# First sweep of a PEER encoder kernel: one 512-column matmul in place of two of 256, the halves added afterwards

## The chip, the cores and the metric

The kernel runs on one core of one Trainium2 chip. The metric is device time in microseconds (us) of one execution. Three runs of the kernel before gave 1670.82, 1672.67 and 1672.75 us, a median of 1672.67 us. Engines are named as the profile names them: PE (TensorE matmul), PEld (its weight load), DVE (VectorE), ACT (ScalarE), POOL (GpSimd), SP (SyncE, which issues the plain loads).

## The reference

One encoder layer over 256 tokens of 2048 values, all in float32: a norm, an input projection, two kinds of attention, an output projection, and then a PEER layer, which is what this case is about. Each token picks 8 x 16 of 16384 experts by two short searches, takes the dot product of its normed row with each chosen expert's row of `peer_u`, puts it through gelu, weighs it, and sums rows of `peer_v`:

```python
q = (xt @ w_query).reshape(n_tok, PEER_HEADS, 2, PEER_QUERY_DIM // 2)
scores = jnp.einsum('thcd,hcnd->thcn', q, sub_keys)
s_top, i_top = lax.top_k(scores, PEER_TOPK)
cand = s_top[:, :, 0, :, None] + s_top[:, :, 1, None, :]
best, pos = lax.top_k(cand.reshape(...), PEER_TOPK)
u = jnp.take(expert_u, eb, axis=0)
act = jax.nn.gelu(jnp.einsum('td,thkd->thk', xb, u))
return jnp.einsum('thk,thkd->td', act * gb, vv)
```

## The kernel before

Float32 products are made of three matmuls on rounded parts. An operand `w` is split by ACT into `hi`, its rounded high part, and by DVE into `lo = w - hi`; a product is `hi*h_hi + hi*h_lo + lo*h_hi`. `load_split` (line 165) takes one unit of 128 x 1024 values: a load of 512 KB on SP's queue, the ACT copy (L169, `hi`) and the DVE subtraction (L170, `lo`). `hi` and `lo` have three buffers each, so the split of a unit waits until PE has finished the unit three before it. Loads go to five raw buffers, three of their own and two in a part of the large array `A` that isn't in use yet.

The kernel is a chain of stages: projections and attention, the query projection (four groups), the first sweep, an extraction stage, the second sweep, the end.

The first sweep (from line 777) multiplies the first 1536 of the 2048 dimensions of all 16384 rows of `peer_u` with all 256 tokens. It has 192 units of 8 blocks of 128 x 128. A group `e` of 128 experts has KA = 12 blocks, so it lasts one and a half units; there are 128 groups. For each block three matmuls of 256 columns run one after the other (L790, L791, L792). `h_hi` and `h_lo` lie side by side in the tile `hTa[:, k]`, 2 x 256 values. Two groups share one PSUM bank (`both`), and when the odd one of a pair is done ACT copies the 512 sums into `A[:, e // 2]` (L795), where the two groups of a pair alternate.

The other 512 dimensions are fetched, not swept: for each token and each chosen expert a "dot" gathers a 2 KB row per partition with an indirect DMA by POOL (L644) and multiplies and sums it on DVE (L650). There are 256 dots. They can start once a query group's search is done. The searches themselves (top 16 of 128, pairs, top 16 of the pairs, decoding) are DVE steps, put in between.

DVE's order is written out by hand in this stretch (`manual_schedule`): per unit first the `lo` subtraction, then whatever `advance()` hands out. `advance()` (called once a unit) gives the searches a share of each unit: the work left divided by the units left until unit SEARCHED, but at most `rate` and at least MIN_S = 1.0, in its own cost units; the dots get what is left of `rate`:

```python
rate = max(rate, RATE)
share = max(min(rate, todo / max(SEARCHED - st["unit"], 1)), MIN_S) if todo else 0
```

Unit 0 of the sweep is unit 33 in that count. Before the searches are done the dots have four row buffers (`wm`). When they are done (`selected`), eight more are opened at once in pairs 52 to 59 of `A`, whose space the searches have used until then. Each buffer in `A` is closed four units before the sweep writes its pair. The row buffers are taken in turn from a queue; a newly opened one is put at its front.

After the sweep, the extraction stage reads all of `A` from its first matmul on (L838).

Of the kernel before, what the change touches and what calls it, by code (L numbers as in the profile page):

```python
# [13 lines left out]
AF = mybir.ActivationFunctionType  # L14
OP = mybir.AluOpType
# [3 lines left out]
P = 128  # L19
D = 2048  # L20
S = 256
# [14 lines left out]
KA = D1 // P  # L36
# [7 lines left out]
WORK = 14016  # L44
SEARCH = 22.0
DOT = 0.67
SEARCHED = 95
MIN_S = 1.0
RATE = 1.42
TAIL = 5  # L50
# [4 lines left out]
PAIRS = (52, 60)  # L55
# [47 lines left out]
def encoder_layer_kernel(ctx: ExitStack, tc: tile.TileContext, x, gT, w_in, gq, gk, w_out, g2,  # L103
                         w_query, sub_keys, u_head, u_tail, v_head, v_tail, gf, cst, rope, bias_a, out):
    nc = tc.nc
# [8 lines left out]
    A = consts.tile([P, NK // 2, S, 2], F32, name="A")  # L114
    arena = A.rearrange("p a b c -> p (a b c)")
    ha_pool = ctx.enter_context(ExitStack())
    hb_pool = ctx.enter_context(ExitStack())
    hTa = ha_pool.enter_context(tc.tile_pool(name="ha", bufs=1)).tile([P, KA, 2, S], F32R, name="hTa")
    hTb = hb_pool.enter_context(tc.tile_pool(name="hb", bufs=1)).tile([P, KD - KA, 2, S], F32R, name="hTb")

    def hTs(k, part, r):
        return hTa[:, k, part, r] if k < KA else hTb[:, k - KA, part, r]
# [15 lines left out]
    def mm_bank(name="mm"):  # L138
        return psm.tile([P, 512], F32, name=name, tag="mm")

    def at_bank(name="at"):
        return psa.tile([P, 512], F32, name=name, tag="at")
# [15 lines left out]
    def load_raw(src):  # L158
        raw = raw_tile("raw")[:, :src.shape[-1]]
        nc.sync.dma_start(raw, src)  # L160
        return raw
# [3 lines left out]
    def load_split(src):  # L165
        raw = loaded.popleft() if loaded else load_raw(src)
        hi, lo = (wp.tile([P, 1024], F32R, name=s, tag=s, bufs=3)[:, :raw.shape[-1]] for s in ("hi", "lo"))
        with tc.high_priority(AHEAD):
            nc.scalar.activation(hi, raw, AF.Copy)  # L169
            nc.vector.tensor_tensor(lo, raw, hi.bitcast(F32), op=OP.subtract)  # L170
        return hi, lo
# [91 lines left out]
    def project(xT, unit, order, background=None):  # L263

        ps = [mm_bank(f"pr{t}") for t in range(NT)]
        for n, i in enumerate(order):
            hi, lo = load_split(unit(i))
            for kk in range(2):
                k = 2 * i + kk
                c = slice(kk * 512, (kk + 1) * 512)  # L270
                first, last = n == 0 and kk == 0, n == len(order) - 1 and kk == 1
                for t in range(NT):
                    r = slice(t * P, (t + 1) * P)
                    nc.tensor.matmul(ps[t], xT(k, 0, r), hi[:, c], start=first, stop=False)  # L274
                    nc.tensor.matmul(ps[t], xT(k, 0, r), lo[:, c], start=False, stop=False)  # L275
                    nc.tensor.matmul(ps[t], xT(k, 1, r), hi[:, c], start=False, stop=last)  # L276
            if background:
                background()
        return ps
# [110 lines left out]
    def w_in_group(g, background=tick):  # L390
        return project(hTs, lambda i: w_in[g, i], W_OUT_ORDER if g == 5 else range(KD // 2), background)
# [3 lines left out]
    def enter():  # L395
        if entries:
            gained_.append(entries.popleft())
            transpose_gain(0, *gained_[-1])

    def split_entered():  # L400
        if gained_:
            t, c = gained_.popleft()
            split_rows(4 * c, 4, slice(t * P, (t + 1) * P))

    with tc.manual_schedule(engines={DVE}):
        for step in (enter, enter, split_entered, split_entered, enter):
            step()
        ps = w_in_group(8, lambda: (split_entered(), enter()))
# [11 lines left out]
    with tc.manual_schedule(engines={PE}):  # L420
# [58 lines left out]
        for g in range(4):  # L479
            ps = project(hTs, lambda i: w_out[g, i], W_OUT_ORDER, tick)  # L480
# [160 lines left out]
    spares = Ring([arena[:, i:i + DT] for i in range(SPARE * S, NK * S, DT)])  # L641
# [45 lines left out]
    def advance():  # L687
        st = state
        st["unit"] += 1
        while known and known[0][0] <= st["unit"]:  # L690
            g = known.popleft()[1]
            dotq.extend((t, 32 * g + j) for t in range(NT) for j in range(32))
        todo = sum(c for c, *_ in searches) + (4 - st["groups"]) * SEARCH
        rate = (todo + DOT * (NT * P - st["dots"])) / max(last_unit - st["unit"], 1)
        if todo:
            rate = max(rate, RATE)
        share = max(min(rate, todo / max(SEARCHED - st["unit"], 1)), MIN_S) if todo else 0
        st["s"] += share
        st["d"] += max(rate - share, 0)
        if not dotq:  # L700
            st["s"] += st["d"]
            st["d"] = 0.0
        while searches and st["s"] >= searches[0][0]:
            cost, fn, *args = searches.popleft()
            fn(*args)
            st["s"] -= cost
        if not searches:
            st["d"] += max(st["s"], 0) if dotq else 0
            st["s"] = 0.0
        while dotq and (st["d"] >= DOT or st["unit"] >= last_unit):  # L710
            dot(*dotq.popleft())
            st["dots"] += 1
            st["d"] -= DOT

    query = ctx.enter_context(ExitStack())
    for g in range(4):
        if g == 1:
            query.enter_context(tc.manual_schedule(engines={DVE}))
        ps = project(hTs, lambda i: w_query[g, i], QUERY_ORDER, advance if g else None)
# [10 lines left out]
    spares = Slots()  # L730
# [8 lines left out]
    def select_transposed(t):  # L739
        rows_ = sel.rearrange("p c g (t h) k -> p c t g (h k)", t=NT)[:, :, t]  # L740
        flat = seln[:, t]
        for c in range(3):
            nc.scalar.activation(flat[:, c].rearrange("p (g j) -> p g j", g=4), rows_[:, c], AF.Copy)
        nc.sync.dma_start(i1d[t * P:(t + 1) * P], flat[:, 0])
        tp = at_bank("seltp")
        for c in range(3):
            nc.tensor.transpose(tp[:, c * P:(c + 1) * P], flat[:, c], ident)
        for c, dst in enumerate((I1T, I2T, GT)):
            nc.scalar.activation(dst[:, t * P:(t + 1) * P], tp[:, c * P:(c + 1) * P], AF.Copy)

    units = NK * KA // 8
    both = None
    partT, actT, wT, wN = (h2t[:, i // 2, i % 2 * S:i % 2 * S + S] for i in range(4))
    wN = wN.rearrange("p (t j) -> p t j", t=NT)
    rootT = part.rearrange("p t j -> p (t j)")
# [3 lines left out]
    def rows_at(q):  # L759

        bc = wp.tile([P, 1024], F32, name="bc", tag="raw", bufs=RAW)
        nc.sync.dma_start(bc, bass.AP(tensor=i1d.tensor, offset=i1d.offset + 4 * q * P, ap=[[0, P], [1, 8 * P]]))
        rows[q // 2] = bc
# [12 lines left out]
    selected = False  # L776
    with query:
        for i in range(units):
            if i == SPARE * KA // 8 - 2:
                del raws[1]  # L780
            hi, lo = load_split(u_head[i])
            for b in range(8):
                e, k = divmod(8 * i + b, KA)
                c = slice(b * P, (b + 1) * P)
                if k == 0:
                    if e % 2 == 0:
                        both = mm_bank("act")
                    ps = both[:, e % 2 * S:e % 2 * S + S]
                h_hi, h_lo = hTs(k, 0, slice(0, S)), hTs(k, 1, slice(0, S))
                nc.tensor.matmul(ps, hi[:, c], h_hi, start=k == 0, stop=False)  # L790
                nc.tensor.matmul(ps, hi[:, c], h_lo, start=False, stop=False)  # L791
                nc.tensor.matmul(ps, lo[:, c], h_hi, start=False, stop=k == KA - 1)  # L792
                if k == KA - 1 and e % 2:
                    with tc.high_priority(FIRST):
                        nc.scalar.activation(A[:, e // 2], both.rearrange("p (c t) -> p t c", c=2), AF.Copy)  # L795
            advance()
            if not searches and not selected:
                selected = True
                for t in range(NT):
                    select_transposed(t)  # L800

                for p in range(PAIRS[1] - 1, PAIRS[0] - 1, -1):
                    spares.add(arena[:, p * 512:(p + 1) * 512], 2 * p * KA // 8 - 4)
            spares.now = i + 1
            if i == READY:
                tp = at_bank("parttp")
                for t in range(NT):
                    nc.tensor.transpose(tp[:, t * P:(t + 1) * P], part[:, t], ident)
                nc.scalar.activation(partT, tp[:, :S], AF.Copy)
                tp = at_bank("roottp")  # L810
                for t in range(NT):
                    nc.tensor.matmul(tp[:, t * P:(t + 1) * P], roots[:, NT + t:NT + t + 1].to_broadcast([P, P]), ident,
                                     start=True, stop=True)
                nc.scalar.activation(rootT, tp[:, :S], AF.Copy)
            if i == units - 1:
                for q in range(0, FULL, 2):
                    rows_at(q)
                for q in range(FULL):
                    hot_at(q)()
# [78 lines left out]
    units = NK * VC // 2  # L898
# [230 lines left out]
```

## Time and profile before

| | |
|---|---|
| median of three runs | 1672.67 us |
| profiled execution | 1670.96 us |
| its span, first to last instruction | 1669.1 us |
| granted TensorE clock, mean | 0.995 |
| PE busy | 1641.6 us (98%) |
| DVE busy | 1319.0 us (79%) |
| ACT busy | 852.9 us (51%) |
| POOL busy | 694.4 us (42%) |
| first sweep, first to last start of L790 | 441.8 to 1008.7 us |

The profiled execution takes 1.9 us more than its span. Busy time of matmuls is modelled at their ends, and matmuls overlap in it, so what a matmul costs in a stream is read from the distance between two starts and not from its duration. Shares of busy time are means over stages with different limits.

### The profile page before, as it was taken

The page shows a single profiled execution, that of the slowest core. Times are in us where ns is not written, and L with a number is a line of the kernel's source. Part 1 is how long each engine was busy: PE and PEld are TensorE (multiplying, and loading weights), DVE is VectorE, ACT ScalarE, POOL GpSimd, SP SyncE. Part 2 cuts the span into 40 slices and gives each one's busy share as a digit, 9 for nine tenths or more (in the row PEclk, how much of TensorE's full clock was granted, in tenths as well). Part 3 has the DMA queues.
Part 4 walks back from the last instruction along what each step waited for, and adds up shares of the span by engine and source line. Part 5 has one row for each costly group of instructions (what it writes and reads, how often), then busy time and mean ns, then how long its engine had stood idle before and what let it go on. Part 6 is the DMA issues. An engine that isn't in the chain of part 4 may idle for free.

```text
span 1669.1 us, 28381 instructions
## 1 busy us (share of the span) xinstructions
PE 1641.6 (98%) x10242; PEld 1489.6 (89%) x10242; DVE 1319.0 (79%) x2902; ACT 852.9 (51%) x1191; POOL 694.4 (42%) x582
## 2 busy tenths in 40 slices
PE   8999999999999999999999999999999999999997
PEld 6888888888899989999999999998888888888886
DVE  6665565569799967777777767997989999999996
ACT  6565564454444434444444448996444444444445
POOL 0000000001223366766765532334777666666661
PEclk9999999999999989999999999999999999999999
DMA  7644565666677789999999973335999999999994
GB/s 254 194 142 153 172 202 164 180 212 211 224 246 235 240 291 325 339 324 335 329 333 310 311 252 130 126 118 183 353 395 363 360 355 344 359 348 357 349 355 151
DMA packets 126173, 443.23 MB, mean 266 GB/s; under 512 B 17744, under 2 KB 18640, under 8 KB 125648
## 3 DMA queue, kind: packets, MB, share of 16 engines
q1 hardware_dynamic: 85072, 298.78, 52.6%
q0 software_dynamic: 40960, 142.64, 24.1%
q8 instruction: 80, 1.31, 0.3%
q14 instruction: 61, 0.50, 0.1%
HBM read 437.02 MB, written 4.33 MB: 264 GB/s over the span
## 4 chain that ended last, share of the span: by engine, by line
PE 92%; DVE 4%; ACT 2%; DMA 1%; issue 1%; SPq 0%; ACTq 0%; DVEq 0%
PE act L791 11%; PE act L790 11%; PE act L792 11%; PE o L924 10%; PE o L925 10%; PE o L923 10%; PE pr L276 6%; PE pr L275 6%; PE pr L274 6%; PE X L838 3%; PE W L888 3%; DVE lo L170 1%; PE o1p L844 1%; PE sc L356 1%; PE po L387 1%
## 5 line engine op out<-in xcount | busy, mean ns | idle before, releaser
L169 ACT ACTIVATE hi<-raw 128x1024 fp32r<-128x1024 f32 (+1 forms) x445 | 464.7, 1045 | 596.6 <-PE o L925 243.1
L170 DVE TENSOR_TENSOR lo<-raw,hi 128x1024 fp32r<-128x1024 f32 (+1 forms) x445 | 535.8, 1204 | 216.5 <-ACT hi L169 189.6
L790 PE MATMUL act<-hTa,hi 128*128 128x256 f32 x1536 | 436.7, 284 | 1.8 <-issue 1.8
L791 PE MATMUL act<-hTa,hi 128*128 128x256 f32 x1536 | 436.7, 284 | 1.8 <-issue 1.8
L792 PE MATMUL act<-hTa,lo 128*128 128x256 f32 x1536 | 436.6, 284 | 0.0
L644 POOL DMA_INDIRECT rows<-in_v_tail_dram,experts x256 | 325.5, 1272 | 152.4 <-DVE vsum L996 88.1
L644 POOL DMA_INDIRECT A<-in_u_tail_dram,experts x131 | 151.2, 1154 | 499.9 <-DVE den L636 408.4
L790 PEld LDWEIGHTS act<-hTa,hi 128*128 128x128 f32 x1536 | 296.6, 193 | 1.6 <-issue 1.5
L792 PEld LDWEIGHTS act<-hTa,lo 128*128 128x128 f32 x1536 | 296.6, 193 | 1.6 <-issue 1.6
L791 PEld LDWEIGHTS act<-hTa,hi 128*128 128x128 f32 x1536 | 296.6, 193 | 1.2 <-issue 1.2
L924 PE MATMUL o<-lo,wt 128*128 128x512 f32 (+1 forms) x768 | 293.5, 382 | 1.0 <-DVE lo L170 0.9
L923 PE MATMUL o<-hi,wt 128*128 128x512 f32 (+1 forms) x768 | 293.5, 382 | 0.9 <-ACT hi L169 0.9
L925 PE MATMUL o<-hi,wt 128*128 128x512 f32 (+1 forms) x768 | 293.2, 382 | 0.0
L644 POOL DMA_INDIRECT wm<-in_u_tail_dram,experts x125 | 160.6, 1285 | 169.1 <-DVE wm L650 120.8
L996 DVE SCALAR_TENSOR_TENSOR vsum<-rows,h2t,vsum 128x576 f32<-128x576 f32 x256 | 208.6, 815 | 11.3 <-DMA rows<-in_v_tail_dram,experts 8.5
L924 PEld LDWEIGHTS o<-lo,wt 128*128 128x128 f32 x768 | 144.3, 188 | 26.0 <-DVE lo L170 1.8
L923 PEld LDWEIGHTS o<-hi,wt 128*128 128x128 f32 x768 | 144.3, 188 | 25.3 <-ACT hi L169 1.4
L925 PEld LDWEIGHTS o<-hi,wt 128*128 128x128 f32 x768 | 144.2, 188 | 24.3 <-DVE wt L918 0.6
L274 PE MATMUL pr<-hi,hTa 128*128 128x512 f32 x408 | 164.3, 404 | 0.0
L275 PE MATMUL pr<-lo,hTa 128*128 128x512 f32 x408 | 160.0, 392 | 0.4 <-DVE lo L170 0.2
L276 PE MATMUL pr<-hi,hTa 128*128 128x512 f32 x408 | 159.6, 391 | 0.0
L169 ACT ACTIVATE hi<-A 128x1024 fp32r<-128x1024 f32 x72 | 76.4, 1062 | 127.5 <-PE act L791 71.1
(160 smaller groups left out, 2073.9 us busy)
## 6 DMA issues: line engine op xcount, KB each, us to landing
raw<-in_v_head_dram SPq DMA_DIRECT2D x128, 512.0 KB
raw<-in_u_head_dram SPq DMA_DIRECT2D x120, 512.0 KB
raw<-in_w_in_dram SPq DMA_DIRECT2D x72, 512.0 KB
A<-in_u_head_dram SPq DMA_DIRECT2D x72, 512.0 KB
raw<-in_v_head_dram SPq DMA_DIRECT2D x64, 448.0 KB
raw<-in_w_out_dram SPq DMA_DIRECT2D x32, 512.0 KB
raw<-in_w_query_dram SPq DMA_DIRECT2D x32, 512.0 KB
bc<-i1d SPq DMA_DIRECT2D x32, 512.0 KB
```

The source lines that it names most:

```text
L169: nc.scalar.activation(hi, raw, AF.Copy)
L170: nc.vector.tensor_tensor(lo, raw, hi.bitcast(F32), op=OP.subtract)
L274: nc.tensor.matmul(ps[t], xT(k, 0, r), hi[:, c], start=first, stop=False)
L275: nc.tensor.matmul(ps[t], xT(k, 0, r), lo[:, c], start=False, stop=False)
L276: nc.tensor.matmul(ps[t], xT(k, 1, r), hi[:, c], start=False, stop=last)
L644: nc.gpsimd.indirect_dma_start(out=rows_, out_offset=None, in_=table, in_offset=bass.IndirectOffsetOnAxis(ap=experts[:, j // 32, t * 32 + ...
L790: nc.tensor.matmul(ps, hi[:, c], h_hi, start=k == 0, stop=False)
L791: nc.tensor.matmul(ps, hi[:, c], h_lo, start=False, stop=False)
L792: nc.tensor.matmul(ps, lo[:, c], h_hi, start=False, stop=k == KA - 1)
L923: nc.tensor.matmul(ps, w[:, 0, r], hi[:, c], start=e == 0, stop=False)
L924: nc.tensor.matmul(ps, w[:, 0, r], lo[:, c], start=False, stop=False)
L925: nc.tensor.matmul(ps, w[:, 1, r], hi[:, c], start=False, stop=e == NK - 1)
```

## The change

- In the first sweep the two matmuls that use the same `hi` block become one of 512 columns over `h_hi` and `h_lo` side by side. The left half of the bank collects `hi*h_hi`, the right half `hi*h_lo`.
- Within a unit, for each group, all 512-column matmuls come first, then the `lo` matmuls of 256 columns, which add to the left half.
- A group has a bank of its own (128 in turn from four, in place of 64). ACT copies the left half (256 values, every second place of `A[:, e // 2]`).
- DVE adds the right half to it in place, three units after the unit in which the group ended, behind that unit's `lo` subtraction and ahead of `advance()`. In the last unit all that are left are added.
- The eight row buffers are opened one in every second unit, from the unit on in which the searches are done.
- SEARCHED goes from 95 to 101.

```diff
-SEARCHED = 95
+SEARCHED = 101
...
-                if k == 0:
-                    if e % 2 == 0:
-                        both = mm_bank("act")
-                    ps = both[:, e % 2 * S:e % 2 * S + S]
-                h_hi, h_lo = hTs(k, 0, slice(0, S)), hTs(k, 1, slice(0, S))
-                nc.tensor.matmul(ps, hi[:, c], h_hi, start=k == 0, stop=False)
-                nc.tensor.matmul(ps, hi[:, c], h_lo, start=False, stop=False)
-                nc.tensor.matmul(ps, lo[:, c], h_hi, start=False, stop=k == KA - 1)
-                if k == KA - 1 and e % 2:
+                blocks.setdefault(e, []).append((k, slice(b * P, (b + 1) * P)))
+            for e, ks in blocks.items():
+                if ks[0][0] == 0:
+                    ps = mm_bank("act")
+                for k, c in ks:
+                    h = (hTa[:, k] if k < KA else hTb[:, k - KA]).rearrange("p a t -> p (a t)")
+                    nc.tensor.matmul(ps, hi[:, c], h, start=k == 0, stop=False)
+                for k, c in ks:
+                    nc.tensor.matmul(ps[:, :S], lo[:, c], hTs(k, 0, slice(0, S)), start=False, stop=k == KA - 1)
+                if ks[-1][0] == KA - 1:
+                    ended.append((i + 3, A[:, e // 2, :, e % 2], ps))
                     with tc.high_priority(FIRST):
-                        nc.scalar.activation(A[:, e // 2], both.rearrange("p (c t) -> p t c", c=2), AF.Copy)
+                        nc.scalar.activation(ended[-1][1], ps[:, :S], AF.Copy)
+            while ended and (ended[0][0] <= i or i == units - 1):
+                _, dst, sums = ended.popleft()
+                nc.vector.tensor_tensor(dst, dst, sums[:, S:], op=OP.add)
             advance()
             if not searches and not selected:
                 selected = True
                 for t in range(NT):
                     select_transposed(t)
-                for p in range(PAIRS[1] - 1, PAIRS[0] - 1, -1):
-                    spares.add(arena[:, p * 512:(p + 1) * 512], 2 * p * KA // 8 - 4)
+                opened = deque(range(*PAIRS))
             spares.now = i + 1
+            if selected and opened and i % 2 == 0:
+                p = opened.popleft()
+                spares.add(arena[:, p * 512:(p + 1) * 512], 2 * p * KA // 8 - 4)
```

## Rows read from the trace of the kernel before

**Rows 1.** The page: PE's busy time, and the chain that ended last.

```profile
PE 1641.6 (98%) x10242; PEld 1489.6 (89%) x10242; DVE 1319.0 (79%) x2902; ACT 852.9 (51%) x1191; POOL 694.4 (42%) x582
PE 92%; DVE 4%; ACT 2%; DMA 1%; issue 1%; SPq 0%; ACTq 0%; DVEq 0%
PE act L791 11%; PE act L790 11%; PE act L792 11%; PE o L924 10%; PE o L925 10%; PE o L923 10%; PE pr L276 6%; PE pr L275 6%; PE pr L274 6%; PE X L838 3%; PE W L888 3%; DVE lo L170 1%; PE o1p L844 1%; PE sc L356 1%; PE po L387 1%
```

**Rows 2.** Busy time by stretch: start:end, length, engines with instruction counts, clock, DMA.

```profile
core 0: us, PE busy (x) PEld busy (x) DVE busy (x) ACT busy (x) POOL busy (x), PEclk, DMA share, GB/s
366.00:400.00 34.00, 33.29 (x166) 26.94 (x165) 30.76 (x122) 17.60 (x23) 0.00 (x0) 1.00 0.49 157
...
452.20:592.00 139.80, 139.80 (x1167) 139.80 (x1167) 128.65 (x381) 60.69 (x70) 46.66 (x32) 1.00 0.75 243
560.00:640.00 80.00, 76.36 (x602) 75.70 (x601) 60.59 (x142) 32.42 (x48) 43.51 (x36) 0.94 0.80 275
600.00:605.00 5.00, 5.00 (x44) 5.00 (x43) 2.50 (x7) 1.89 (x8) 4.09 (x4) 1.00 1.02 403
605.00:610.00 5.00, 3.04 (x22) 2.77 (x22) 1.92 (x3) 1.11 (x2) 3.78 (x5) 0.96 0.93 322
...
615.00:620.00 5.00, 5.00 (x26) 5.00 (x26) 4.36 (x9) 2.17 (x3) 1.95 (x2) 0.51 0.36 108
700.00:900.00 200.00, 200.00 (x1669) 200.00 (x1668) 153.06 (x297) 85.34 (x93) 132.12 (x113) 1.00 0.94 331
1200.00:1400.00 200.00, 200.00 (x914) 171.43 (x913) 183.39 (x211) 92.09 (x102) 141.59 (x109) 1.00 0.99 365
```

**Rows 3.** PE's timeline in the first sweep: start us, duration us, instruction.

```profile
799.82 0.28 PE L792 MATMUL act<-hTa,lo 128*128 128x256 f32 x1
...
821.90 0.28 PE L790 MATMUL act<-hTa,hi 128*128 128x256 f32 x1
```

**Rows 4.** PE's timeline in the second sweep, a run of 512-column matmuls.

```profile
1301.37 0.39 PE L923 MATMUL o<-hi,wt 128*128 128x512 f32 x1
...
1306.60 0.39 PE L925 MATMUL o<-hi,wt 128*128 128x512 f32 x1
```

**Rows 5.** PE's timeline in an input projection, a run of 512-column matmuls.

```profile
101.21 0.39 PE L275 MATMUL pr<-lo,hTa 128*128 128x512 f32 x1
...
103.52 0.40 PE L276 MATMUL pr<-hi,hTa 128*128 128x512 f32 x1
```

**Rows 6.** DVE's timeline in the first sweep while the searches run.

```profile
519.84 1.23 DVE L170 TENSOR_TENSOR lo<-A,hi 128x1024 fp32r<-128x1024 f32 x1 [0.36 <-ACT hi L169]
520.98 0.75 DVE L620 TENSOR_TENSOR A<-A 128x256 f32<-128x256 f32 x2
521.65 0.68 DVE L650 SCALAR_TENSOR_TENSOR wm<-wm,h2t 128x512 f32<-128x512 f32 x1
```

**Rows 7.** Groups by line and shape: count, busy us, mean ns, idle before.

```profile
L326 DVE TENSOR_TENSOR A<-A 128x256 f32<-128x256 f32 x8 | 3.1, 420 | 0.0
L476 DVE TENSOR_TENSOR A<-A,pr 128x512 f32<-128x512 f32 x8 | 5.1, 680 | 0.0
L388 ACT ACTIVATE A<-po 128x256 f32<-128x256 f32 x16 | 6.0, 374 | 0.7 <-PE po L387 0.7
L795 ACT ACTIVATE A<-act 128x512 f32<-128x512 f32 x64 | 37.1, 580 | 1.8 <-PE act L792 1.8
```

**Rows 8.** POOL's timeline where the eight row buffers open.

```profile
602.83 0.95 POOL L644 DMA_INDIRECT A<-in_u_tail_dram,experts  x1 [0.30 <-issue]
...
611.76 0.95 POOL L644 DMA_INDIRECT A<-in_u_tail_dram,experts  x1 [0.30 <-issue]
```

**Rows 9.** SP's timeline of the same stretch.

```profile
606.91 10.32 SPq L160 DMA_DIRECT2D A<-in_u_head_dram  x2
```

**Rows 10.** PE's timeline of the same stretch.

```profile
613.77 0.38 PE L791 MATMUL act<-hTa,hi 128*128 128x256 f32 x1 [1.12 <-issue]
```

**Rows 11.** PE's timeline where the first sweep ends.

```profile
1009.88 1.16 PE L838 MATMUL X<-A,hot 128*128 128x128 f32 x8 [0.69 <-ACT A L795]
```

More of the change, by code (lines that the diff above doesn't have):

```diff
@@ L751, in encoder_layer_kernel @@
     units = NK * KA // 8
-    both = None
+    ended = deque()
     partT, actT, wT, wN = (h2t[:, i // 2, i % 2 * S:i % 2 * S + S] for i in range(4))
@@ L781, in encoder_layer_kernel @@
             hi, lo = load_split(u_head[i])
+            blocks = {}
             for b in range(8):
                 e, k = divmod(8 * i + b, KA)
-                c = slice(b * P, (b + 1) * P)
-                if k == 0:
-                    if e % 2 == 0:
-                        both = mm_bank("act")
-                    ps = both[:, e % 2 * S:e % 2 * S + S]
-                h_hi, h_lo = hTs(k, 0, slice(0, S)), hTs(k, 1, slice(0, S))
-                nc.tensor.matmul(ps, hi[:, c], h_hi, start=k == 0, stop=False)
-                nc.tensor.matmul(ps, hi[:, c], h_lo, start=False, stop=False)
-                nc.tensor.matmul(ps, lo[:, c], h_hi, start=False, stop=k == KA - 1)
-                if k == KA - 1 and e % 2:
+                blocks.setdefault(e, []).append((k, slice(b * P, (b + 1) * P)))
[9 more added lines that the diff above has]
+                    ended.append((i + 3, A[:, e // 2, :, e % 2], ps))
                     with tc.high_priority(FIRST):
-                        nc.scalar.activation(A[:, e // 2], both.rearrange("p (c t) -> p t c", c=2), AF.Copy)
+                        nc.scalar.activation(ended[-1][1], ps[:, :S], AF.Copy)
+            while ended and (ended[0][0] <= i or i == units - 1):
+                _, dst, sums = ended.popleft()
+                nc.vector.tensor_tensor(dst, dst, sums[:, S:], op=OP.add)
             advance()
```

## The prediction

> **What bounds the kernel now.** I read the page first, then the busy time by stretch, then the timelines of the stretches that the change touches. PE is busy for 98% of the span and carries 92% of the chain that ended last; the three lines of the first sweep (L790 to L792) are 33% of it [rows 1]. So the sweep is worth what its matmuls cost in a stream. A busy PE is not yet a full one, but the starts show it: from 799.82 to 821.90 us there are 184 steps of 256 columns without a gap, 22.08/184 = 0.1200 us each [rows 3]. A block of three is 0.360 us, a unit of eight 2.880 us, 192 units 553 us. In two places PE is not alone. While the searches run, DVE is busy 128.65 of 139.80 us, 92%, against 76.5% later (153.06 of 200) [rows 2]. And at 605 to 620 us PE stalls: it is busy 3.04 of 5 us, and then its clock is granted at 0.51, the lower of its two levels, 1.2 in place of 2.4 GHz [rows 2].
>
> **The change part by part.** The sum is made against the profiled execution, 1670.96 us (span 1669.1 and 1.9 around it); the median of the runs is 1.71 us above it.
>
> *One 512 for two 256.* The columns stay the same; what goes is one matmul of three. A 512-column matmul with weights of its own takes (1306.60 - 1301.37)/23 = 0.2274 us in the second sweep [rows 4] and (103.52 - 101.21)/10 = 0.231 us in the projection [rows 5], against 2 x 0.1200 = 0.2400 now. That is 12.6 or 9.0 ns a block. I take the longer run, 12.6. A unit then needs 8 x (0.2274 + 0.1200) = 2.779 us, 0.101 less than now. Over all 192 units that would be 19.4 us (13.8 by the other row). The `lo` matmuls keep their 256 columns and their weight loads, so they keep 0.120.
>
> The Trainium skill (TensorE: Matmul & The Clock Gate, "Back-to-back issue gap") gives an isolated matmul N/2.4 ns and a fixed 2.5 ns more. By it a block would fall by 2.5 ns only, 3.8 us in the whole sweep. The rows have about 14 ns over the 512 columns' 213.3 and 13 over the 256 columns' 106.7, so here the fixed part is several times the page's, and the rows decide.
>
> *The adds on DVE.* 128 tensor-tensor operations of 128x256 are new, one from PSUM and with every second place of `A` as an operand. At that size an operation with a step of two takes 420 ns; 512 elements with an operand in PSUM take 680, so 256 more elements cost 260 and PSUM makes no visible price [rows 7]. In a dense run the ends overlap: two operations of 256 start at 520.98 and the next at 521.65, 0.335 each [rows 6]. Two thirds of an add a unit is 0.223 us (0.280 by the full 420).
>
> After the searches DVE needs 153.06/200 x 2.880 = 2.204 us a unit [rows 2], then 2.43 of 2.779, 87%: hidden. There the gain is whole: 139 units (53 to 191) x 0.101 = 14.0 us.
>
> During the searches it isn't hidden. DVE needs 128.65/139.80 x 2.880 = 2.650 us a unit now and 2.873 then: above PE's new 2.779 and just under its old 2.880. DVE's order is fixed, so what is queued behind an add is the unit's search step and dot and then the next `lo`, which PE waits for. Two things soften it. `lo` can be two units ahead less 1.06 and 1.14 us for the two halves of the split, some 3.4 us, and it is needed 0.9 to 1.8 us later, since the 512-column matmuls come first. The excess is 53 x (2.873 - 2.779) = 5.0 us. If the lead covers all of it, the stretch gains 53 x 0.101 = 5.3 us; if none, 0.4; if an add costs its full 0.42 us and no lead helps, it loses 53 x 0.049 = 2.6. Search steps come in bursts (units with two steps), which eat the lead, so I take 2.0.
>
> *SEARCHED.* A later unit should spread the searches; worked through `advance()` it doesn't. At unit 9 the work left is 20.75 + 3 x 22 = 86.75 units of cost: divided by 95 - 9 that is 1.009, by 101 - 9 it is 0.943, and MIN_S lifts the second to 1.0. As each search costs 20.75 where 22 is held for it, the quotient stays at or under the floor later. Unit by unit, both values hand out the same steps and the same dots, and the searches end in sweep unit 52 with either. Cost and gain: nothing.
>
> *The row buffers.* At 602.83 to 611.76 us POOL issues eight gathers in a row, 1.28 us apart, with nothing to wait for [rows 8]; DMA moves 403 GB/s at a full share [rows 2]; two loads of SP take 10.32 us [rows 9]; PE waits up to 1.12 us at a time [rows 10] and then runs at half clock. From 560 to 640 us there are 602 matmuls listed, six of them transposes: 596 x 0.120 + 0.8 = 72.3 of 80 us, so the stall costs 7.7 us. Opened one by one, the dots keep POOL to one gather ahead more in every second unit. What may come next: in the 16 units of opening DMA has to move 512 KB of load, 1.63 gathers (113 in 200 us [rows 2]) and half a gather more of 256 KB each, 1.08 MB in 2.779 us or 389 GB/s. The rows reach 403 for 5 us and 365 for 200, with PE full [rows 2]. So gathers may fall behind, by 16 x (2.96 - 2.779) = 3 us in all (1.08 MB at 365 GB/s take 2.96 us). I count 7.0 of the 7.7 as gained; the bounds are 0 and 7.7.
>
> *Banks, ACT, the end.* ACT goes from 64 copies of 0.580 to 128 of about 0.374 us [rows 7], 10.7 us more in the sweep, beside the splits, with ACT busy 43% of the time (85.34 of 200 [rows 2]): hidden. A bank is wanted again four groups later, in the fifth unit after its group ended; its add stands behind the `lo` of the third, ahead of that of the fourth, which PE needs before: no wait. At the end the last group's copy (0.374 in place of 0.580) is followed by its add (0.42) and a signal between engines, where now PE's first extraction matmul follows the copy after 0.69 us of idle time [rows 11]: 0.4 us lost, 0.2 to 0.6.
>
> **Sum**: 14.0 + 2.0 + 7.0 - 0.4 = 22.6 us. 1670.96 - 22.6 = 1648.4 as the profiled execution, 1650.1 at the level of the median: 1650.
>
> **The rivals.**
>
> *DVE never binds and the stall goes whole*: 19.4 + 7.7 - 0.4 = 26.7, so 1646. For it: the lead of two units about equals the excess. Against it: the bursts, and a DVE at 92% now.
>
> *The stall stays*: gathers in the queue still push the loads aside at the moment when DVE has no lead left: 22.6 - 7.0 = 15.6, so 1657. For it: 389 GB/s wanted. Against it: the loads lost their turn to eight gathers in a row, which the new order can't issue.
>
> *Transfers bind after the searches*: units stay at 2.880 us and the 14.0 go: 8.6, so 1664. For it: a DMA share of 0.94 at 331 GB/s, and the new pace wants 343. Against it: the second sweep moves 365 with PE busy throughout [rows 2]. The Trainium skill (DMA: Bandwidth & Descriptors, "Where 436 GB/s comes from") has the limit of HBM for a core at about 358 GB/s; the 365 and 403 of the rows lie above it.
>
> *The fused matmul saves nothing*: over `hTa` a 512-column matmul takes the 0.240 us of two of 256, so only the buffers' 7.0 less 0.4 at the end are left: 6.6, so 1666. The 0.2274 and 0.231 of two other stages speak against it [rows 4, 5]. The Trainium skill's rule above would put it some 3 us lower, at 1663, by the same mechanism.
>
> *Slower: DVE paces PE and the clock falls.* Place: the 53 units of the searches. Waits for `lo` break PE's stream, the clock goes to its lower level as at 615 to 620 us, where PE lists 26 matmuls in 5 us and not 44 [rows 2]. At half rate each us loses half of itself, so beyond 45 us of it the 22.6 are gone; 60 us give 1670.96 - 22.6 + 30 + 1.7 = 1680. Against it: from 366 to 400 us DVE is busy 30.76 of 34 us and paces PE (33.29), and the clock stays at 1.00 [rows 2]; and a slow PE would let DVE get ahead again.
>
> **How the numbers follow.** Chances: the forecast 0.52 (its own range 1645 to 1655), DVE hidden 0.18, the stall stays 0.12, transfers bind 0.09, nothing saved 0.03, slower 0.06. The range reaches down past the full 19.4 and 7.7 and up to the case of bound transfers: 1643 to 1664. About 0.2%, 3.3 us, is what a measurement here can tell from no change. Faster holds for all but the slower case and the part of the case of bound transfers in which the stall stays as well (1671): 0.90 faster, 0.04 the same, 0.06 slower.
>
> **What would show it.** Starts of 512-column matmuls in the sweep 0.227 to 0.231 us apart and of `lo` ones 0.120, a unit of 2.78 us after the searches. DVE near 100% from 452 to 592 us, with idle PE ahead of `lo` matmuls and a pace near 2.84 us a unit. The last search step still in unit 52. No run of eight gathers, no load of 10 us, and a clock of 1.00 around 600 us. An add of about 0.42 us. I'm wrong if the fused matmul takes 0.24, if PE stands still around unit 52 all the same, or if a DMA wait stands ahead of `hi` after it.

## The result, and the profile after

Four executions of the changed kernel took 1658.01, 1658.1, 1659.56 and 1661.08 us, a median of 1658.83 us; four of the kernel before beside them had a median of 1672.55. The ratio is 0.9922 (95% interval 0.991 to 0.9934): faster by 13 us. The forecast was 1650 in a range of 1643 to 1664, and what came nearest is the rival "the stall stays" at 1657. The profiled execution took 1659.56 us (span 1657.8), 11.4 less than the one before.

The page after, PE's busy line and the chain [rows 1]:

```profile
PE 1627.9 (98%) x8706; PEld 1408.2 (85%) x8706; DVE 1358.7 (82%) x3030; ACT 867.1 (52%) x1255; POOL 705.2 (43%) x582
PE 94%; DVE 2%; DMA 1%; ACT 1%; issue 1%; SPq 0%; ACTq 0%; DVEq 0%
```

PE lists 1536 matmuls fewer (10242 - 8706), one for each block of the sweep. DVE lists 128 instructions more, the adds.

PE's timeline after the searches, merged runs of the two kinds (start, duration, instruction, count), to be read with [rows 3]:

```profile
804.08 2.00 PE L792 MATMUL act<-hTa,hi 128*128 128x512 f32 x8
805.92 1.11 PE L794 MATMUL act<-hTa,lo 128*128 128x256 f32 x8
806.87 2.00 PE L792 MATMUL act<-hTa,hi 128*128 128x512 f32 x8
...
943.96 1.09 PE L792 MATMUL act<-hTa,hi 128*128 128x512 f32 x4
```

From start to start eight fused matmuls take 1.84 us, 0.230 each, and eight `lo` ones 0.95, 0.119 each, 2.79 us for this unit. From 804.08 to 943.96 us there are 50 units, (943.96 - 804.08)/50 = 2.798 us each in place of 2.880: 0.082 less.

Busy time by stretch, with the columns of [rows 2]:

```profile
452.00:592.00 140.00, 140.00 (x803) 122.94 (x802) 139.55 (x420) 65.97 (x92) 55.82 (x34) 1.00 0.72 249
600.00:605.00 5.00, 4.56 (x23) 3.26 (x22) 2.40 (x7) 0.40 (x1) 3.78 (x5) 1.00 1.01 394
605.00:610.00 5.00, 2.62 (x10) 1.45 (x9) 0.56 (x2) 1.06 (x1) 3.40 (x4) 0.99 0.92 325
610.00:615.00 5.00, 4.07 (x12) 3.31 (x12) 4.44 (x8) 2.59 (x4) 2.03 (x2) 0.50 0.60 187
615.00:620.00 5.00, 5.00 (x27) 4.56 (x27) 5.00 (x12) 2.31 (x3) 3.83 (x4) 0.82 0.91 325
700.00:900.00 200.00, 200.00 (x1146) 175.62 (x1146) 173.34 (x354) 93.36 (x120) 142.16 (x115) 1.00 0.96 339
```

While the searches run DVE is busy 139.55 of 140 us, as good as always, and PE loses nothing by it. The stall is still there: from 605 to 610 us PE is busy 2.62 of 5 us, and only after that the granted clock falls to 0.50, its lower level. PE's timeline shows how it looks from within:

```profile
604.77 0.39 PE L792 MATMUL act<-hTa,hi 128*128 128x512 f32 x1 [0.21 <-issue]
605.50 0.72 PE L792 MATMUL act<-hTa,hi 128*128 128x512 f32 x2 [0.34 <-issue]
...
608.36 0.28 PE L794 MATMUL act<-hTa,lo 128*128 128x256 f32 x1 [0.90 <-issue]
609.07 0.50 PE L794 MATMUL act<-hTa,lo 128*128 128x256 f32 x2 [0.44 <-issue]
...
611.19 0.37 PE L794 MATMUL act<-hTa,lo 128*128 128x256 f32 x1 [0.93 <-issue]
611.36 3.62 PE L792 MATMUL act<-hTa,hi 128*128 128x512 f32 x8
```

One or two matmuls start every 0.7 us or a multiple of it, and what ended each gap is not a load, ACT or DVE but "issue": nothing that the profile shows. I call this the slow issue. At 611.36 the stream goes on at once, at half clock.

POOL and SP in the same stretch [rows 8, 9]. POOL's gathers follow each other without a wait from 587.85 to the first of these rows, 16 of them; then SP's row, two issues of a load:

```profile
608.36 0.95 POOL L644 DMA_INDIRECT wm<-in_u_tail_dram,experts  x1 [0.30 <-issue]
612.67 1.16 POOL L644 DMA_INDIRECT A<-in_u_tail_dram,experts  x1 [3.36 <-DVE A L650]
```

```profile
604.64 7.50 SPq L160 DMA_DIRECT2D A<-in_u_head_dram  x2
```

Opening the buffers one by one did not break up POOL's run of gathers: in the kernel before 15 of them follow each other in the same way, from 592.25 to 611.76 us.

To divide the 11.3 us of the spans' difference I use two marks that each kernel has once: the transposes right behind the last search step (`seltp`) and the first matmul of the extraction (`X`). First and last starts stand behind the durations; after:

```profile
L747 PE MATMUL seltp<-cs,A x6: 270/272/273, 593.7 to 594.2; 128*128 128x128 f32 x6
L846 PE MATMUL X<-A,hot x512: 270/273/378, 993.3 to 1124.3; 128*128 128x128 f32 x171
```

All executions with a profile, read in the same way (us; the sweep's first matmul is at 440.0 to 442.8 in all of them). A row is one execution, and in five versions (before with two opened, and changed with eight at once, two opened, dots later and none opened) it is the fastest of its set:

| kernel | seltp | X | seltp to X | X to end | slow issue, 600 to 620 us? |
|---|---|---|---|---|---|
| before | 599.3 | 1009.9 | 410.6 | 659.2 | yes |
| before, again | 601.3 | 1011.4 | 410.1 | 662.2 | yes |
| before, buffers one by one | 598.5 | 1009.6 | 411.1 | 660.8 | yes |
| before, two opened | 596.8 | 1001.6 | 404.8 | 659.6 | no |
| changed | 593.7 | 993.3 | 399.6 | 664.5 | yes |
| changed, again | 594.6 | 986.0 | 391.4 | 663.7 | no |
| changed, third | 593.9 | 985.2 | 391.3 | 664.0 | no |
| changed, eight at once | 593.1 | 990.9 | 397.8 | 660.6 | yes |
| changed, two opened | 593.6 | 984.9 | 391.3 | 661.8 | no |
| changed, two opened, again | 595.3 | 986.6 | 391.3 | 661.5 | no |
| changed, dots later | 592.4 | 983.9 | 391.5 | 659.6 | no |
| changed, none opened | 593.2 | 999.6 | 406.4 | 662.7 | no |
| changed, `lo` block by block | 594.6 | 991.0 | 396.4 | 662.9 | no (PE waits 1.0 us for `lo`) |
| changed, adds doubled | 602.9 | 1001.1 | 398.2 | 663.3 | no (PE waits 2.3 us for `lo`) |

Between the first row and "changed": the sweep starts 0.8 us earlier (441.0 for 441.8), the searches' stretch gains 4.8 (152.7 for 157.5), the rest of the sweep 11.0, and from X to the end 5.3 are lost.

### The profile page after: what moved, and what is told of

It reads as the page before. It is cut to its first block, busy times and chain, and to the rows that moved or that the text cites. A ratio compares the mean times of both kernels' runs of the same rounds, so it can differ in the third digit from the quotient of the medians.

```text
span 1657.8 us, 25499 instructions
## 1 busy us (share of the span) xinstructions
PE 1627.9 (98%) x8706; PEld 1408.2 (85%) x8706; DVE 1358.7 (82%) x3030; ACT 867.1 (52%) x1255; POOL 705.2 (43%) x582
## 4 chain that ended last, share of the span: by engine, by line
PE 94%; DVE 2%; DMA 1%; ACT 1%; issue 1%; SPq 0%; ACTq 0%; DVEq 0%
PE act L792 21%; PE act L794 11%; PE o L932 10%; PE o L933 10%; PE o L931 10%; PE pr L275 7%; PE pr L276 7%; PE pr L274 7%; PE X L846 3%; PE W L896 3%; PE o1p L852 1%; PE sc L356 1%; PE po L387 1%; DMA raw<-in_v_head_dram 1%; DVE lo L170 1%
## 5 line engine op out<-in xcount | busy, mean ns | idle before, releaser
L792 PE MATMUL act<-hTa,hi 128*128 128x512 f32 x1536 | 399.3, 395 | 0.8 <-issue 0.8
L644 POOL DMA_INDIRECT rows<-in_v_tail_dram,experts x256 | 321.1, 1254 | 161.7 <-DVE vsum L1004 96.0
L644 POOL DMA_INDIRECT A<-in_u_tail_dram,experts x128 | 158.5, 1239 | 471.9 <-DVE den L636 408.6
L792 PEld LDWEIGHTS act<-hTa,hi 128*128 128x128 f32 x1536 | 272.7, 190 | 46.9 <-issue 2.2
L794 PEld LDWEIGHTS act<-hTa,lo 128*128 128x128 f32 x1536 | 219.5, 191 | 24.5 <-issue 3.5
L644 POOL DMA_INDIRECT wm<-in_u_tail_dram,experts x128 | 168.0, 1313 | 166.7 <-DVE wm L650 122.3
L794 PE MATMUL act<-hTa,lo 128*128 128x256 f32 x1536 | 226.5, 283 | 3.0 <-issue 3.0
L170 DVE TENSOR_TENSOR lo<-A,hi 128x1024 fp32r<-128x1024 f32 x72 | 88.3, 1227 | 27.0 <-ACT hi L169 17.3
L889 POOL TENSOR_SCALAR o<-cs,I2T,h2t 128x128 f32<-128x128 f32 x64 | 54.9, 862 | 114.5 <-DVE h2t L880 56.2
```

Of the source, the lines that this page charges most:

```text
L644: nc.gpsimd.indirect_dma_start(out=rows_, out_offset=None, in_=table, in_offset=bass.IndirectOffsetOnAxis(ap=experts[:, j // 32, t * 32 + ...
L792: nc.tensor.matmul(ps, hi[:, c], h, start=k == 0, stop=False)
L794: nc.tensor.matmul(ps[:, :S], lo[:, c], hTs(k, 0, slice(0, S)), start=False, stop=k == KA - 1)
```

## The experiments

My theory: the faster matmul gives its 0.08 us in every unit, DVE hides the adds, and the stall is a matter of the row buffers. The rivals: the gain is the buffers'; or the stall comes from something else.

**The buffers alone.** The kernel before with nothing but the new opening:

```diff
-                for p in range(PAIRS[1] - 1, PAIRS[0] - 1, -1):
-                    spares.add(arena[:, p * 512:(p + 1) * 512], 2 * p * KA // 8 - 4)
+                opened = deque(range(*PAIRS))
...
+            if selected and opened and i % 2 == 0:
+                p = opened.popleft()
+                spares.add(arena[:, p * 512:(p + 1) * 512], 2 * p * KA // 8 - 4)
```

> The kernel before with one edit alone: the eight row buffers open one in every second unit. In the trace of the changed kernel PE still stands still for some 7.5 us right after the searches, and POOL still issues eleven gathers in a row there. Theory A (gathers): 1.63 dots a unit and half a gather of opening a unit already keep POOL at its full pace, so opening one by one holds nothing back: the stall stays at 7 to 8 us and the time within 1.5 us of before, 1672. Rival (the stall of the changed kernel is a new one, made by a DVE without lead): here DVE has its lead, the stall goes, 1665.

Measured: 1670.77 us (1665.82 to 1675.54, 10 runs), ratio 0.9995 (0.9981 to 1.001). The profile has the stall, at 612.7 to 620 us. So opening one by one is worth nothing that can be measured, and the gain must come from the matmuls. The ten times spread over 9.7 us, those of the kernel before beside them over 4.5 (1668.54 to 1673.07, 19 runs), and the two at 1666 us have a mean granted clock of 0.997 and 0.998, the profiled one 0.994. So the stall may come and go here too; no profile shows it.

**The matmuls with the old opening.** The changed kernel, all eight opened at once:

```diff
-                opened = deque(range(*PAIRS))
+                for p in range(PAIRS[1] - 1, PAIRS[0] - 1, -1):
+                    spares.add(arena[:, p * 512:(p + 1) * 512], 2 * p * KA // 8 - 4)
```

> The changed kernel with the eight row buffers opened at once again. Theory A (gathers): a stall of 7 to 10 us at the end of the searches as now, time within 2 us of the changed kernel, 1657 to 1661. Rival (opening one by one did save some of it, and something else took it back): the stall grows by 3 us or more, 1662 or more.

Measured: 1655.04 us (1653.28 to 1658.36, 4 runs), ratio 0.9909 (0.9891 to 0.9926): the gain is there without the new opening. The stall too, and it cost 6.4 us (397.8 - 391.4, the way from seltp to X of the same matmuls without a stall, below).

**No buffers opened.** `opened = deque()` in the changed kernel, so that the dots keep their four.

> The changed kernel with none of the eight row buffers opened; the four in wm serve all dots. Theory A (the stall comes from POOL gathering far ahead of DVE): with four buffers POOL must wait for DVE, DMA at 590 to 620 us falls under a full share, the stall shrinks from 7.5 to under 2 us, 1651 to 1653. Rival 1 (the stall comes from what ends the searches itself, its transposes and its writes, whatever the gathers do): stall and time as in the changed kernel, 1657 to 1661. Rival 2 (four are too few): DVE waits for gathers in every unit and PE for DVE, 1662 or more.

Measured: 1669.9 us (1664.08 to 1675.33, 10 runs), ratio 0.9996 (0.9986 to 1.0006). The slow issue is not in this profile: PE is busy 25.00 of 25 us from 595 to 620. But DVE now waits for gathers, and the way from seltp to X grows to 406.4 us, in an execution that is 5.8 us faster than the median. DVE's waits on gathers in the whole profile:

```profile
DVE wm L650 <- DMA wm<-in_u_tail_dram,experts: 61.8, 56, 3.0
```

61.8 us in 56 waits. Four buffers are too few: what the faster matmuls gain is lost to dots that come late.

**Block by block.** The changed kernel with each block's `lo` matmul right behind its fused one:

```diff
                 for k, c in ks:
                     h = (hTa[:, k] if k < KA else hTb[:, k - KA]).rearrange("p a t -> p (a t)")
                     nc.tensor.matmul(ps, hi[:, c], h, start=k == 0, stop=False)
-                for k, c in ks:
                     nc.tensor.matmul(ps[:, :S], lo[:, c], hTs(k, 0, slice(0, S)), start=False, stop=k == KA - 1)
```

> The changed kernel with the matmul of lo right behind the fused matmul of its block. It has the same matmuls. If the order that puts all 512-column matmuls first is what keeps PE from waiting for DVE during the searches (lo is needed 0.9 to 1.8 us later), PE gets idle time ahead of lo between 452 and 595 us, 1 to 3 us in all: 1660 to 1662. If two units of lead are enough by themselves: within 1 us of the changed kernel, and a unit stays at 2.79 us.

Measured: 1654.71 us (1652.7 to 1661.22, 4 runs), ratio 0.9907 (0.9879 to 0.9936). PE waits for `lo` twice: 0.2 us in the stretch of the searches, and 1.0 us at 605, behind a gather that DVE waited 1.75 us for. One row of its busy time, to be compared with 1146 matmuls in 200 us above:

```profile
700.00:800.00 100.00, 100.00 (x568) 86.67 (x567) 86.74 (x175) 45.59 (x60) 61.49 (x58) 1.00 0.95 338
```

568 in 100 us are 2.82 us a unit of 16, where 1146 in 200 are 2.79: 0.03 a unit, some 4 us over 139 units, which with the 1.0 us accounts for its 396.4 us against 391.4. So having all 512-column matmuls first helps a little by the stream itself. It isn't what keeps PE from waiting for `lo` during the searches.

**The changed kernel again**, without an edit.

> The changed kernel itself, on the same chip as the next three, as their measure: 1655 to 1661, PE standing still for 4 to 8 us in the trace some 10 us after the searches, in waits that name no engine.

Measured: 1653.51 us (1650.55 to 1659.12, 4 runs), ratio 0.9889 (0.9859 to 0.992). The surprise is in its profile. Busy time by stretch, to be compared with the 600 to 615 us of the first profile of this kernel:

```profile
600.00:605.00 5.00, 5.00 (x31) 4.41 (x30) 1.90 (x5) 1.46 (x2) 3.78 (x5) 1.00 1.01 394
605.00:610.00 5.00, 5.00 (x31) 4.43 (x30) 5.00 (x12) 3.42 (x5) 4.08 (x4) 1.00 0.89 297
610.00:615.00 5.00, 5.00 (x31) 4.44 (x30) 4.96 (x11) 2.62 (x4) 4.09 (x4) 1.00 0.95 329
```

The same instructions, the same 394 GB/s at a share of 1.01 from 600 to 605 us, as many gathers by POOL, which goes on from 586 to 640 us without once waiting for a buffer for more than its own 0.3 us; and PE doesn't stall. Seltp to X takes 391.4 us, so the stall in the first profile cost 399.6 - 391.4 = 8.2 us.

**Two buffers opened in place of eight**, the rest as in the changed kernel:

```diff
-PAIRS = (52, 60)
+PAIRS = (52, 54)
```

> The changed kernel with two row buffers opened in place of eight: six in all. Theory B (POOL's run: PE's stall lasts as long as POOL issues gathers back to back with nothing to wait for, 18 of them after the searches): six buffers make POOL wait for DVE after some ten, the stall falls under 3 us, and six are enough for DVE: 4 to 7 us less than the changed kernel. Rival (the searches' end makes the stall): no difference to the changed kernel. Other rival: six are too few as four were, DVE waits for gathers and PE for lo, slower than the changed kernel.

Measured: 1649.23 us (1648.5 to 1651.58, 4 runs), ratio 0.9859 (0.9838 to 0.9881). No slow issue, 391.3 us from seltp to X.

**Dots later.** The changed kernel with the dots held back for some units after the searches:

```diff
         if todo:
             rate = max(rate, RATE)
+        elif st["unit"] < 97:
+            rate = min(rate, 0.42)
```

> The changed kernel with the dots held to their old pace (0.42 of budget a unit) for 12 more units after the searches; then they go at 1.8 a unit. The buffers open as in the changed kernel. Theory B (POOL's run): POOL needs 1.1 gathers a unit while the buffers open and never runs for long at its full pace: the stall at 600 to 612 us goes, 4 to 8 us less than the changed kernel. If the run merely moves, a stall stands at 630 to 650 us. Rival (the end of the searches itself, its transposes and writes): the stall stays at 600 to 612 us.

Measured: 1650.4 us (1645.26 to 1651.23, 4 runs), ratio 0.9863 (0.9842 to 0.9884). No slow issue either, with eight buffers: 391.5 us. The profile is that of the 1645.26, 4.4 us below the next.

**Adds doubled.** Each add is issued twice, so that the output has the right halves of the sums twice:

```diff
                 nc.vector.tensor_tensor(dst, dst, sums[:, S:], op=OP.add)
+                nc.vector.tensor_tensor(dst, dst, sums[:, S:], op=OP.add)
```

> The changed kernel with every add done twice; the sums are wrong by the right half. DVE is busy 59.83 of 60 us there while the searches run, and yet PE shows no wait. Theory (PE's pace there just equals DVE's, the lead covered the rest): 0.223 us more a unit of DVE work, 53 units, leaves nothing to cover it: PE waits for lo between 452 and 600 us, 8 to 12 us in all, so 8 to 12 us more than the changed kernel; after the searches DVE goes to 95% and hides it. Rival (DVE has slack that its busy time does not show): under 3 us more.

Measured: 1668.45 us (1663.87 to 1671.06, 10 runs), ratio 0.9969 (0.9958 to 0.9981); 15 us above the changed kernel beside it, more than the 8 to 12 expected. Now PE waits: seltp comes at 602.9 us, 8.3 later than in the changed kernel beside it (594.6), and from 441 to 610 us the waits for `lo` are

```profile
PEld act L794 <- DVE lo L170: 14.9, 24, 1.7
PE act L794 <- DVE lo L170: 5.3, 10, 1.3
```

and the stretch of the searches reads

```profile
500.00:560.00 60.00, 56.59 (x309) 46.52 (x309) 59.39 (x182) 25.12 (x34) 20.28 (x12) 1.00 0.66 225
```

DVE sets the pace, with the clock at 1.00. After the searches the added work is hidden (DVE 97.08 of 100 us from 700 to 800, PE 574 matmuls). The way to X is 6.8 us longer as well (398.2 for 391.4), and not by slow issue: behind the searches PE stands still three times, and the longest stop is a wait for a `lo` that DVE made late because it waited for a gather:

```profile
618.31 1.21 PE L794 MATMUL act<-hTa,lo 128*128 128x256 f32 x8 [2.31 <-issue]
```

```profile
616.41 0.69 DVE L650 SCALAR_TENSOR_TENSOR wm<-wm,h2t 128x512 f32<-128x512 f32 x1 [2.58 <-DMA wm<-in_u_tail_dram,experts]
617.03 0.08 DVE L650 DVE_READ_ACCUMULATOR wm<-wm,h2t 128x1 f32 x1
617.03 1.22 DVE L170 TENSOR_TENSOR lo<-A,hi 128x1024 fp32r<-128x1024 f32 x1
```

The eight `lo` matmuls start together at 618.31, as DVE's `lo` ends (617.03 + 1.22), and the clock stays at 1.00. The other two stops, at 635.71 and 639.73 us, are 1.35 us together; the rest of the 6.8 I did not divide. So in the changed kernel DVE has room for its one add a group, though it is busy all the time, and not for a second.

**Is the stall in the kernel before each time, and is it the buffers' number?** Four runs beside each other. The kernel before, unchanged:

> The kernel before itself, for a second profile. Theory A (its stall is there in every execution, since all of its times lie at 1668 to 1676): seltp to extraction again 409 to 412 us, matmuls with slow issue around 600 to 620 us, ratio 1.000. Theory B (the stall comes and goes here too, and other things make up for it): no such matmuls in this profile and about 403 us.

Measured: 1672.29 us (1670.52 to 1675.37, 11 runs), ratio 1.0002 (0.9993 to 1.0011). The stall is there again:

```profile
605.00:610.00 5.00, 4.67 (x38) 4.37 (x36) 1.52 (x2) 1.54 (x2) 3.78 (x5) 1.00 0.97 368
610.00:615.00 5.00, 2.19 (x11) 1.63 (x11) 0.41 (x2) 0.00 (x0) 4.05 (x4) 0.97 0.91 316
615.00:620.00 5.00, 4.81 (x20) 4.52 (x21) 2.40 (x6) 2.00 (x2) 0.30 (x1) 0.50 0.45 106
```

The kernel before with `PAIRS = (52, 54)` and nothing else:

> The kernel before with two row buffers opened after the searches (pairs 52 and 53, both at once) in place of eight; the three matmuls stay. Theory A (the stall of about 7 us behind the searches comes from having many row buffers at once, and has nothing to do with the matmuls): the stall goes here too, the way from seltp to the extraction falls from 410.6 us to about 403, and the time to about 1665, ratio 0.995 to 0.997. Theory B (the stall goes only together with the faster matmuls, or six buffers are too few for the old order): the time stays within 2 us of the kernel before.

Measured: 1664.71 us (1662.94 to 1670.2, 9 runs), ratio 0.9966 (0.9954 to 0.9978). The stall is gone in the profile, in the same stretch:

```profile
605.00:610.00 5.00, 5.00 (x44) 5.00 (x43) 4.25 (x10) 2.04 (x3) 3.02 (x4) 1.00 0.94 320
610.00:615.00 5.00, 5.00 (x44) 5.00 (x43) 3.84 (x7) 1.84 (x4) 2.80 (x3) 1.00 0.87 287
```

So fewer buffers are worth 1671.61 - 1664.71 = 6.9 us to the kernel before (1671.61 is the median of the 20 runs beside it), about the size of its stall, without any change to the matmuls.

The changed kernel a third time:

> The changed kernel once more, beside the version with two buffers. In one of its two profiles the stall was there (seltp to extraction 399.6 us, 1659.6 us in all), in the other it wasn't (391.4 us, 1651.5 us). Theory A (the stall is there in some executions of the changed kernel and not in others): times between 1650 and 1661, a median of 1653 to 1659. Theory B (the stall is a property of the chip or of the day): all times lie together at one of the two ends.

Measured: 1651.46 us (1650.77 to 1654.08, 4 runs), ratio 0.9885 (0.987 to 0.99); no stall in the profile. All four lie at the lower end, so this set by itself speaks for the second theory; the set before it, 1650.55 to 1659.12 on one chip, speaks for the first. Over three sets this kernel's twelve times reach from 1650.55 to 1661.08, and the profiled 1659.56, with the stall, and 1651.49 and 1651.01, without it, mark the two ends.

Two buffers opened, again:

> The changed kernel with two row buffers opened in place of eight, again. Theory A (fewer buffers keep the stall out in every execution): all times between 1647 and 1653, ratio to the kernel before 0.985 to 0.988, some 4 to 6 us under the median of the changed kernel. Theory B (the four executions without a stall were luck): a spread like that of the changed kernel, up to 1660.

Measured: 1649.32 us (1646.92 to 1649.86, 4 runs), ratio 0.9862 (0.9848 to 0.9877). Of eight executions with two buffers none is above 1651.58. This version has the lowest median in both of its sets; beside the changed kernel it is 4.3 and 2.1 us faster, and the intervals overlap in both, so that it is faster than the changed kernel is likely and not shown.

Not run: the changed kernel with SEARCHED at 95. With 95 the program is the same to the last instruction, so there is nothing to time.

## Why the prediction was right, and where it was wrong

*One 512 for two 256: right, a little too high.* The fused matmul takes 0.230 us in the unit shown, near the dearer of the two rows that I had (0.231 [rows 5] against 0.2274 [rows 4], which I took). 0.082 a unit over 139 units are 11.4 us, not 14.0. The Trainium skill (TensorE: Matmul & The Clock Gate, "Back-to-back issue gap") has 2.5 ns above N/2.4; 0.230 us is some 17 ns above the 213.3, so the trace disagrees here.

*The adds: mechanism right, size wrong to the low side.* An add takes what was read from other rows. The groups, with mean ns, and DVE's timeline:

```profile
L801 DVE TENSOR_TENSOR A<-A,act 128x256 f32<-128x256 f32 x128 | 53.3, 416 | 7.4 <-ACT A L798 7.4
L798 ACT ACTIVATE A<-act 128x256 f32<-128x256 f32 x128 | 51.0, 399 | 87.4 <-PE act L794 58.6 <-issue 24.0 <-remote 4.7
```

```profile
521.88 0.42 DVE L801 TENSOR_TENSOR A<-A,act 128x256 f32<-128x256 f32 x1
522.21 1.29 DVE L620 TENSOR_TENSOR A<-A 128x512 f32<-128x512 f32 x2
```

416 ns by itself (420 taken) and 0.33 to the next start (0.335 taken). DVE became as full as I said. But I let it cost 3.3 of 5.3 us, and it cost nothing: the stretch gained 4.8, no less than 53 x 0.082 = 4.3. PE shows no wait for `lo` in it, so the lead of two units covered whatever DVE fell behind. The doubled adds show the edge: a second add of the same size takes 8.3 us from the stretch.

*SEARCHED: right*, it does nothing.

*Banks and ACT: right.* ACT's copies take 0.399 us (0.374 taken), and from the searches to the end of the sweep PE waits for nothing but the stall.

*The row buffers: this step failed*, by one of the prediction's own signs: PE stood still around unit 52 all the same. I counted 7.0 us for opening them one by one, and alone it gave a ratio of 0.9995 (0.9981 to 1.001). The size of the stall was right (6.9 us by the version with two buffers, 8.2 in the first profile of the changed kernel); the remedy and the cause were not. "Opened one by one, the dots keep POOL to one gather ahead more in every second unit" takes the order of the program for an order in time. A buffer that is free carries no wait, so POOL runs through the openings ahead of the sweep, as the 16 gathers without a wait show; and the "eight gathers in a row" of before were 15. And "the loads lost their turn to eight gathers in a row" was no cause: the profile without the stall has the same gathers and the same 394 GB/s. Nor do PE's own rows ever name a load. The 10.32 us [rows 9] are not the time that two loads take: the row runs from one issue of 0.33 us to the end of the next, and between them SP waited 9.6 us for DVE's `lo`, the last to read the raw buffer. I took an effect of the stall for its cause, and passed over the "issue" in [rows 10]. SP's waits for DVE in the kernel before, 595 to 620 us (total, times, longest):

```profile
SPq L160 <- DVE lo L170: 16.8, 4, 9.6
```

What is shown: with two buffers the stall stays away in all three profiles (one before, two changed) and the times of the changed kernel with them are close together; with eight it is in all three profiles with the old matmuls; with the new ones and eight buffers it comes and goes from execution to execution (of the unchanged program one profile has it and two do not). With the dots held back it is not in the one profile that there is. In all five profiles that have it PE's stream is back 1 to 2 us after the last gather of POOL's run has ended (before: 613.77 and 612.71 us; changed: 611.19 and 609.31), and the run ended because DVE, behind PE, freed no more rows. That and the profiles with two buffers speak for a part of the gathers in it; the second profile of the changed kernel, with as long a run and no stall, says that they are not enough. What stays open is why PE issues slowly then. It isn't late data: in the first profile of the changed kernel only the first `lo` of the unit has to wait for anything, and the matmuls behind it come just as slowly. Nor does it show as late instructions: the trace's `instruction` queue has no transfer between the first and the last slow matmul of any of the five profiles.

*The end of the sweep: right in size.* PE's row at the start of the extraction [rows 11]:

```profile
993.29 1.16 PE L846 MATMUL X<-A,hot 128*128 128x128 f32 x8 [0.94 <-DVE A L801]
```

0.94 us of idle time behind the add for 0.69 behind the copy, and 0.4 was forecast for both copy and add.

*What wasn't in the sum: the start of the second sweep.* From X to the end the first profile lost 5.3 us. PE's timeline, where its first `hi` is late:

```profile
1149.64 0.74 PE L931 MATMUL o<-hi,wt 128*128 128x448 f32 x1 [3.91 <-ACT hi L169]
1150.77 0.74 PE L932 MATMUL o<-lo,wt 128*128 128x448 f32 x1 [0.39 <-DVE lo L170]
1151.31 0.57 PE L933 MATMUL o<-hi,wt 128*128 128x448 f32 x1
```

The wait of 3.91 us is followed by matmuls at the lower clock (0.57 us each). The wait is 0.9 us in the first profile of the kernel before, 3.0 in its second, and 3.3 to 3.9 in the three of the changed kernel. X to the end is 659.2 and 662.2 in the one and 663.7 to 664.5 in the other. But the wait is 2.1 us with eight opened at once (660.6) and 0.5 with the dots later (659.6), with the same matmuls and adds. The four profiles with the old matmuls have 659.2 to 662.2 us, the ten with the new ones 659.6 to 664.5, so a loss by the change is not shown, and what sets the wait stays open.

*The sum again.* In an execution without a stall: 5 in the searches, 11.4 behind them, 7 for the stall and -3 at the second sweep (664 against a mean of 660.7) are 20.4 us, and the third set measured 1671.61 - 1651.46 = 20.2. With the stall 7 or 8 of these are missing, which is the first set's 1658.8. The forecast of 1650 describes the first case; it came out 9 us low since the 7.0 has nothing behind it but the execution's luck. That the 1658.8 lies in the range is no merit of the sum: the range was made wide enough for rivals, of which "the stall stays" came nearest.

*The other rivals.* "Transfers bind after the searches" fell: 339 GB/s at a share of 0.96 with PE full from 700 to 900 us, and 380 GB/s over 620 to 640 us of the second profile. The Trainium skill (DMA: Bandwidth & Descriptors, "Where 436 GB/s comes from") has about 358 GB/s as a core's limit of HBM; the 380 lie above it. "DVE never binds and the stall goes whole" (1646) had the right first half. "DVE paces PE" needs twice the adds, and even then the clock stayed at 1.00.

## What to carry to other kernels

Two matmuls that share their weights are worth joining when the fixed cost of a matmul shows in the starts of a stream; here the dearer of two rows was the right one for the joined matmul. An engine at 99.7% is not yet the bound if what others take from it is ready units ahead: doubling the added work shows how far the edge is. Opening buffers later in the program doesn't hold back an engine that runs ahead of it; only a buffer that is still in use does. And a long row of the DMA queue can be two short issues with a wait between them.

## What the hardware showed that I had not expected

PE can issue one or two matmuls per 0.7 us with its data ready, in a stretch where gathers and loads fill the DMA engines (394 GB/s at a share of 1.01), and can run through the same stretch at full pace in another execution of the same program. It costs 6 to 8 us, the granted clock's fall to 0.50 behind it included; why it happens is open. And the order of matmuls counts in a stream without waits: 512 and 256 columns in turn take 2.82 us a unit, eight of the one and then eight of the other 2.79.
